# Rotary embedding: the middle batches moved in pairs, 32 KB to a partition

## The chip, the core and the metric

The kernel runs on one core of a Trainium2 chip. Times are device microseconds, with the other cores idle. The span is the profiled execution from the first to the last instruction; the time of the same execution is a little longer (161.94 against 160.5 us in the profiled run of the kernel before). Every ratio below is to runs of the kernel before that were made on the same chip in the same rounds; where the times or traces of two changed kernels are set side by side, they come from different chips unless the text says otherwise. A run of one core is called slow when it took over 1.5% more than the fastest run of the same kernel, the other runs "fast". A difference under 2% counts as "the same".

Names: VectorE (DVE in the profile), GpSimd (POOL), TensorE (PE, with PEld for its weight loads), ScalarE (ACT), SyncE (SP). A line number such as L224 is a line of that kernel's source.

## The reference

```python
# x: (16, 512, 1024) float32, 16 heads of 64; cos, sin: (512, 32)
x = x.reshape(batch, seq, num_heads, head_dim)
x1, x2 = x[..., :half_dim], x[..., half_dim:]
rotated = concatenate([x1 * cos - x2 * sin, x1 * sin + x2 * cos], axis=-1)
```

32 MiB come in and 32 MiB go out. cos and sin depend on the position in the sequence only, so every batch uses the same tables.

## The kernel before

A partition holds 4 consecutive positions ("rows") of a batch: 16 KB that are contiguous in memory. One load and one store of 2 MB serve a batch. For each row VectorE multiplies by cos into PSUM (`mul`), GpSimd multiplies the swapped halves by sin into `t2`, and then the two are added: by VectorE (`comb`), or for 3 rows in 8 by TensorE (an identity matrix times `t2`, accumulated onto the cos product in PSUM), in which case ScalarE copies the sum back. For one row in 8, VectorE also makes the sin product itself.

```python
PE2 = [u % 8 in (1, 3, 6) for u in range(NU)]   # u: rows in order; TensorE adds these
V2 = [u % 8 == 3 for u in range(NU)]            # VectorE makes the sin product of these
NT1 = 3                                         # PSUM slots for cos products
LEAD = 2
...
def on_sync(sp):                                # loads, 10 batches ahead of the stores
    for c in range(NC):
        if c * R >= RING:
            sp.wait_ge(sem_out[c - RING // R], 16)
        sp.dma_start(tile(c), xv[c]).then_inc(sem_in[c], 16)
...
def on_scalar(ae):
    for u in range(NU):
        if PE2[u]:
            ae.wait_ge(sem_e, n_pe[u])
            ae.activation(xs[:, k, :], t1_ps[:, u % NT1, :], COPY).then_inc(sem_a, 1)
        if r == R - 1:                          # last row of the batch
            wait_added(ae, u)
            ae.dma_start(ov[c], tile(c))...     # store
...
def mul(u):                                     # VectorE
    if r == 0:
        ve.wait_ge(sem_in[c], 16)
    if V2[u]:
        ve.tensor_tensor(t2_sb[...], swapped(k), sin_of(s_ps, r), mult)
    if u >= NT1:                                # the PSUM slot of row u - 3 must be free
        ve.wait_ge(sem_a, ...) if PE2[u - NT1] else ve.wait_ge(sem_v, ...)
    ve.tensor_tensor(t1_ps[:, u % NT1, :], x_sb[...], c_ps[...], mult)
...
for u in range(NU + LEAD):                      # VectorE's order: mul(u), then comb(u - 2)
    if u < NU:
        mul(u)
    if u >= LEAD and not PE2[u - LEAD]:
        comb(u - LEAD)
```

## Time and profile before

The median of the first three runs was 161.89 us, of six runs 162.0 us (161.85 to 162.4). The span of the profiled run was 160.5 us.

| what | before |
|---|---|
| DMA, mean over the span | 419 GB/s, full from 8 to 155 us |
| VectorE, GpSimd busy | 82%, 81% |
| GpSimd waits for loads | 8.9 us |
| VectorE waits for ScalarE (a PSUM slot) | 8.6 us |

Lines of the profile page of the kernel before: busy time of the engines, the DMA rows of the span in 40 slices (busy share in tenths, then GB/s), the packets, and three groups of instructions (busy us and mean ns of one, then idle time before them and what ended most of it).

```profile
span 160.5 us, 607 instructions
PE 81.7 (51%) x102; PEld 25.4 (16%) x102; DVE 131.5 (82%) x116; ACT 26.3 (16%) x27; POOL 130.3 (81%) x62
DMA  5999999999999999999999999999999999999996
GB/s 151 404 445 429 433 429 404 412 441 421 433 445 416 441 433 418 441 421 437 431 425 441 421 441 425 433 437 420 441 429 429 433 425 441 429 429 437 421 435 290
DMA packets 4899, 67.27 MB, mean 419 GB/s; under 512 B 544, under 2 KB 800, under 8 KB 800
...
L193 POOL TENSOR_TENSOR t_sb<-x_sb,s_sb 128x1024 f32<-128x1024 f32 x56 | 129.6, 2376 | 17.0 <-DMA x_sb<-in_x_dram 8.9
L224 DVE TENSOR_TENSOR t_ps<-x_sb,tab_ps 128x1024 f32<-128x1024 f32 x64 | 77.1, 1227 | 10.4 <-ACT x_sb L141 8.6
L235 DVE TENSOR_TENSOR x_sb<-t_ps,t_sb 128x1024 f32<-128x1024 f32 x40 | 48.6, 1217 | 0.0
```

The DMA engines do not pause (a share of 1.00 to 1.03 in every stretch of the table from 8 to 155 us). GpSimd has room, and what it waits for is loads. The table by stretches of the kernel before (busy us of each engine, granted TensorE clock, DMA share, GB/s) has a middle piece and the piece near the end:

```profile
core 0: us, PE busy (x) PEld busy (x) DVE busy (x) ACT busy (x) POOL busy (x), PEclk, DMA share, GB/s
60.00:80.00 20.00, 11.38 (x15) 3.14 (x13) 19.64 (x18) 4.09 (x4) 20.00 (x10) 0.71 1.01 431
...
144.20:150.80 6.60, 2.93 (x4) 0.83 (x4) 5.84 (x5) 1.30 (x2) 3.79 (x2) 0.69 1.00 429
```

### The profile page before, as it was taken

What the parts mean: (1) busy time and instruction counts of PE and PEld (TensorE: products, weight loads), DVE (VectorE), ACT (ScalarE), POOL (GpSimd) and SP (SyncE); (2) the same over time, 40 slices, a digit from 0 to 9 for tenths busy, and PEclk for the clock granted to TensorE, in tenths of its full rate; (3) what the DMA queues carried; (4) which work ended last, traced back from release to release, by engine and by line L of the source; (5) the groups of instructions that cost most, each with busy time, mean ns of one, the idle gap of its engine ahead of it and who ended that gap; (6) DMA issues with size and microseconds to landing.
All of it is one profiled execution on the core that took longest, in us unless ns stands there. A gap on an engine that the chain in (4) does not pass through costs nothing.

```text
span 160.5 us, 607 instructions
## 1 busy us (share of the span) xinstructions
PE 81.7 (51%) x102; PEld 25.4 (16%) x102; DVE 131.5 (82%) x116; ACT 26.3 (16%) x27; POOL 130.3 (81%) x62
## 2 busy tenths in 40 slices
PE   6004928354833944854573584575485436576000
PEld 1002402110210220211022021122022002112000
DVE  0089299999999879999999699998999799969400
ACT  3010221122022022012202202211211220220200
POOL 1069999999999999999999993998939988498000
PEclk9999996879595558595765555765567795567555
DMA  5999999999999999999999999999999999999996
GB/s 151 404 445 429 433 429 404 412 441 421 433 445 416 441 433 418 441 421 437 431 425 441 421 441 425 433 437 420 441 429 429 433 425 441 429 429 437 421 435 290
DMA packets 4899, 67.27 MB, mean 419 GB/s; under 512 B 544, under 2 KB 800, under 8 KB 800
## 3 DMA queue, kind: packets, MB, share of 16 engines
q1 hardware_dynamic: 2592, 33.69, 49.9%
q10 hardware_dynamic: 2304, 33.56, 48.8%
q14 instruction: 3, 0.02, 0.0%
HBM read 33.69 MB, written 33.55 MB: 419 GB/s over the span
## 4 chain that ended last, share of the span: by engine, by line
DVE 36%; PE 19%; issue 17%; POOL 10%; ACT 5%; DMA 5%; SPq 0%; DVEq 0%; POOLq 0%
PE t_ps L164 19%; DVE x_sb L235 18%; DVE t_ps L224 15%; POOL t_sb L193 10%; ACT x_sb L141 5%; DMA stage<-in_sin_dram 5%; DVE t_sb L215 4%; SPq L127 0%; SPq L124 0%; ACT s_sb L135 0%; ACT s_sb L136 0%; DVEq L234 0%; DVEq L223 0%; POOLq L116 0%; DVEq L221 0%
## 5 line engine op out<-in xcount | busy, mean ns | idle before, releaser
L193 POOL TENSOR_TENSOR t_sb<-x_sb,s_sb 128x1024 f32<-128x1024 f32 x56 | 129.6, 2376 | 17.0 <-DMA x_sb<-in_x_dram 8.9
L164 PE MATMUL t_ps<-t_sb,ident 128*128 128x512 f32 x96 | 78.9, 972 | 65.8 <-DVE t_ps L224 49.8
L224 DVE TENSOR_TENSOR t_ps<-x_sb,tab_ps 128x1024 f32<-128x1024 f32 x64 | 77.1, 1227 | 10.4 <-ACT x_sb L141 8.6
L235 DVE TENSOR_TENSOR x_sb<-t_ps,t_sb 128x1024 f32<-128x1024 f32 x40 | 48.6, 1217 | 0.0
L141 ACT ACTIVATE x_sb<-t_ps 128x1024 f32<-128x1024 f32 x24 | 24.6, 1023 | 115.8 <-PE t_ps L164 100.9
L164 PEld LDWEIGHTS t_ps<-t_sb,ident 128*128 128x128 f32 x96 | 24.7, 281 | 119.4 <-DVE t_ps L224 86.4
L215 DVE TENSOR_TENSOR t_sb<-x_sb,tab_ps 128x1024 f32<-128x1024 f32 x8 | 9.7, 1210 | 0.0
L202 DVE COPY tab_ps<-stage 128x128 f32<-128x128 f32 x1 | 0.3, 294 | 7.6 <-DMA stage<-in_cos_dram 7.6
L150 PE MATMUL t_ps<-zero 128*128 128x512 bf16 x6 | 2.7, 630 | 1.3 <-DVE zero L198 1.3
L135 ACT ACTIVATE s_sb<-stage 128x128 f32<-128x128 f32 x1 | 0.3, 309 | 6.9 <-DMA stage<-in_sin_dram 6.9
L135 ACT ACT_TABLE_LOAD x1 | 1.3, 1283 | 0.8 <-PEq L268 0.8
L150 PEld LDWEIGHTS t_ps<-zero 128*128 128x128 bf16 x6 | 0.7, 137 | 2.4 <-DVE zero L198 1.2
L198 DVE MEMSET zero<- 128x256 uint32 x1 | 0.3, 272 | 0.9 <-PEq L268 0.9
L175 POOL MEMSET ident<- 128x128 f32 x1 | 0.2, 204 | 0.3 <-POOLq L268 0.3
L177 POOL TENSOR_SCALAR_AFFINE_SELECT ident<-ident 128x128 f32<-128x128 f32 x1 | 0.3, 292 | 0.1
L268 POOL MEMSET const-float32-0.0<- 128x1 f32 x1 | 0.1, 98 | 0.3 <-issue 0.3
L136 ACT ACTIVATE s_sb<-stage 128x128 f32<-128x128 f32 x1 | 0.3, 293 | 0.0
L204 DVE TENSOR_SCALAR tab_ps<-stage 128x128 f32<-128x128 f32 x1 | 0.3, 283 | 0.0
L205 DVE COPY tab_ps<-stage 128x128 f32<-128x128 f32 x1 | 0.3, 283 | 0.0
L268 POOL MEMSET const-bfloat16-1.0<- 128x1 bf16 x1 | 0.1, 101 | 0.0
L268 POOL MEMSET const-uint8-127<- 128x1 uint8 x1 | 0.1, 101 | 0.0
L268 POOL MEMSET const-float32-1.0<- 128x1 f32 x1 | 0.1, 98 | 0.0
## 6 DMA issues: line engine op xcount, KB each, us to landing
x_sb<-in_x_dram SPq DMA_DIRECT2D x16, 2048.0 KB, 52.5
out_dram<-x_sb ACTq DMA_DIRECT2D x16, 2048.0 KB, 19.3
stage<-in_cos_dram SPq DMA_DIRECT2D x1, 64.0 KB, 7.5
stage<-in_sin_dram SPq DMA_DIRECT2D x1, 64.0 KB, 7.2
```

Of the source, the lines that this page charges most:

```text
L135: ae.activation(s_sb[:, :, 0, :], sv, COPY, scale=-1.0)
L136: ae.activation(s_sb[:, :, 1, :], sv, COPY).then_inc(sem_s, 1)
L141: ae.activation(xs[:, k, :], t1_ps[:, u % NT1, :], COPY).then_inc(sem_a, 1)
L150: pe.matmul(t1_ps[:, k, b * BANK:(b + 1) * BANK], zero[:, 0:P], zero[:], start=True, stop=True).then_inc(sem_w, 1)
L164: ins = pe.matmul(t1_ps[:, u % NT1, b * BANK:(b + 1) * BANK], ident[:], t2[:, b * BANK:(b + 1) * BANK], start=False, stop=True, skip_group ...
L177: pl.affine_select(out=ident[:], in_=ident[:], compare_op=mybir.AluOpType.is_equal, fill=0.0, base=0, pattern=[[-1, P]], channel_multiplier=1,
L193: pl.tensor_tensor(t2_sb[:, u % NT2, :, :, :], swapped(k), sin_of(s_sb, r), mult).then_inc(sem_p, 1)
L198: ve.memset(zero[:], 0.0).then_inc(sem_z, 1)
L215: ve.tensor_tensor(t2_sb[:, u % NT2, :, :, :], swapped(k), sin_of(s_ps, r), mult).then_inc(sem_d, 1)
L224: ve.tensor_tensor(t1_ps[:, u % NT1, :].rearrange("p (h d) -> p h d", d=HALF), x_sb[:, k, :, :, :].rearrange("p h t d -> p (h t) d"), c_ps ...
L235: ve.tensor_tensor(xs[:, k, :], t1_ps[:, u % NT1, :], t2_sb[:, u % NT2, :, :, :].rearrange("p h t d -> p (h t d)"), add,).then_inc(sem_v, 1)
L268: nc = _bacc.Bacc("TRN2", target_bir_lowering=False, num_devices=1)
```

## The change

Packets of 32 KB instead of 16 KB should cost the DMA engines less overhead: an estimate from the transfer records of the kernel before, where a line through 27 ns for 512 B and 611 ns for 16 KB leaves 8 ns for a packet itself. 32 KB contiguous bytes are 8 rows, so a batch covers only 64 partitions, and batches 1 to 14 are taken in pairs: partition p holds 8 rows of batch p % 2 of the pair. Batches 0 and 15 stay single, to keep the start and the end short. The pairs need tables in another arrangement; TensorE makes them at the start, by multiplying the single tables with two selection matrices. Core of the diff:

```diff
-    PE2 = [u % 8 in (1, 3, 6) for u in range(NU)]
-    V2 = [u % 8 == 3 for u in range(NU)]
+    tiles = [(0, R1)] + [(b, R2) for b in range(1, batch - 1, 2)] + [(batch - 1, R1)]   # R1 = 4, R2 = 8
+    REGIONS = 5
+    def on_pe(t, r):
+        return r in {0: (1,), NT - 1: (1, 3)}.get(t, (1, 3, 6))
+    V_ROW = {NT - 1: 1}
+    V2 = [t > 0 and r == V_ROW.get(t, 3) for t, r in rows]
...
-        xv = x.rearrange("b (p r) d -> b p (r d)", r=R)
+        x1 = x.rearrange("b (s r) d -> b s (r d)", r=R1)
+        x2 = x.rearrange("b (s r) d -> s b (r d)", r=R2)
...
-                sp.dma_start(tile(c), xv[c]).then_inc(sem_in[c], 16)
+                sp.dma_start(in_sbuf(t), in_dram(x1, x2, t)).then_inc(sem_in[t], 16)   # 4 MB for a pair
...
-                if r == R - 1:
+                if r == tiles[t][1] - 1:          # a pair's store only after its 8th row
                     wait_added(ae, u)
-                    ae.dma_start(ov[c], tile(c))...
+                    ae.dma_start(in_dram(o1, o2, t), in_sbuf(t))...
...
+            for k in range(2):                    # tables of the pairs
+                pe.matmul(pair_ps[:, k]..., pick[:, k]..., stage[:]..., start=True, stop=True)
```

Two things ride along. Loads and stores of the pairs become ready in steps of 4 MB. And the rows were dealt out anew at the ends: VectorE's own sin product moved from row 3 of batch 0 to row 1 of batch 15.

More of the change, by code (lines that the diff above doesn't have):

```diff
@@ L26, in bass_split_heads_rope_kernel @@
     P = 128
-    R = 4
-    assert P * R == seq
+    R1 = seq // P
+    R2 = 2 * R1
+    assert R1 * P == seq and R1 == 4 and batch % 2 == 0
     fp32 = mybir.dt.float32
@@ L34, in bass_split_heads_rope_kernel @@
     COPY = mybir.ActivationFunctionType.Copy
-    RING = 40
-    NC = batch
-    NU = batch * R
-    def where(u):
-        return u // R, u % R, u % RING
-    PE2 = [u % 8 in (1, 3, 6) for u in range(NU)]
-    V2 = [u % 8 == 3 for u in range(NU)]
+    tiles = [(0, R1)] + [(b, R2) for b in range(1, batch - 1, 2)] + [(batch - 1, R1)]
+    NT = len(tiles)
+    REGIONS = 5
+    rows = [(t, r) for t, (_, n) in enumerate(tiles) for r in range(n)]
+    NU = len(rows)
+    def on_pe(t, r):
+        return r in {0: (1,), NT - 1: (1, 3)}.get(t, (1, 3, 6))
+    V_ROW = {NT - 1: 1}
+    PE2 = [on_pe(t, r) for t, r in rows]
+    V2 = [t > 0 and r == V_ROW.get(t, 3) for t, r in rows]
     def count(flags):
@@ L61, in bass_split_heads_rope_kernel @@
     with ExitStack() as stack:
-        x_sb = stack.enter_context(nc.sbuf_tensor([P, RING, H, 2, HALF], fp32))
+        x_sb = stack.enter_context(nc.sbuf_tensor([P, REGIONS * R2, H, 2, HALF], fp32))
         t2_sb = stack.enter_context(nc.sbuf_tensor([P, NT2, H, 2, HALF], fp32))
-        stage = stack.enter_context(nc.sbuf_tensor([P, 2, R * HALF], fp32))
-        s_sb = stack.enter_context(nc.sbuf_tensor([P, R, 2, HALF], fp32))
+        stage = stack.enter_context(nc.sbuf_tensor([P, 2, R1 * HALF], fp32))
+        s1_sb = stack.enter_context(nc.sbuf_tensor([P, R1, 2, HALF], fp32))
+        s2_sb = stack.enter_context(nc.sbuf_tensor([P, R2, 2, HALF], fp32))
         ident = stack.enter_context(nc.sbuf_tensor([P, P], fp32))
+        pick = stack.enter_context(nc.sbuf_tensor([P, 2, P // 2, 2], fp32))
         zero = stack.enter_context(nc.sbuf_tensor([P, BANK], bf16))
         tab_ps = stack.enter_context(nc.psum_tensor([P, BANK], fp32))
+        pair_ps = stack.enter_context(nc.psum_tensor([P, 2, 2, R1, HALF], fp32))
         t1_ps = stack.enter_context(nc.psum_tensor([P, NT1, H * HD], fp32))
-        sem_in = [stack.enter_context(nc.semaphore(f"in{c}")) for c in range(NC)]
-        sem_out = [stack.enter_context(nc.semaphore(f"out{c}")) for c in range(NC - RING // R)]
+        sem_in = [stack.enter_context(nc.semaphore(f"in{t}")) for t in range(NT)]
+        sem_out = [stack.enter_context(nc.semaphore(f"out{t}")) for t in range(NT - REGIONS)]
         sem_rest = stack.enter_context(nc.semaphore("rest"))
@@ L84, in bass_split_heads_rope_kernel, with c_of, s_of, in_dram @@
         sem_e = stack.enter_context(nc.semaphore("pe"))
+        sem_g = stack.enter_context(nc.semaphore("pick"))
+        sem_t = stack.enter_context(nc.semaphore("pairs"))
         sem_a = stack.enter_context(nc.semaphore("act"))
-        c_ps = tab_ps[:, 0:R * HALF].rearrange("p (r d) -> p r d", d=HALF)
-        s_ps = tab_ps[:, R * HALF:R * (HALF + HD)].rearrange("p (r t d) -> p r t d", t=2, d=HALF)
-        xv = x.rearrange("b (p r) d -> b p (r d)", r=R)
-        ov = out.rearrange("b (p r) h d -> b p (r h d)", r=R)
-        xs = x_sb[:].rearrange("p n h t d -> p n (h t d)")
-        def tile(c):
-            k = c * R % RING
-            return x_sb[:, k:k + R].rearrange("p n h t d -> p (n h t d)")
+        c1_ps = tab_ps[:, 0:R1 * HALF].rearrange("p (r d) -> p r d", d=HALF)
+        v_ps = tab_ps[:, R1 * HALF:R1 * HALF + 2 * HD].rearrange("p (k t d) -> p k t d", t=2, d=HALF)
+        def c_of(t, r):
+            return c1_ps[:, r, :] if tiles[t][1] == R1 else pair_ps[:, r // R1, 0, r % R1, :]
+        def s_of(t, r):
+            return s1_sb[:, r] if tiles[t][1] == R1 else s2_sb[:, r]
+        x1 = x.rearrange("b (s r) d -> b s (r d)", r=R1)
+        o1 = out.rearrange("b (s r) h d -> b s (r h d)", r=R1)
+        x2 = x.rearrange("b (s r) d -> s b (r d)", r=R2)
+        o2 = out.rearrange("b (s r) h d -> s b (r h d)", r=R2)
+        xs = x_sb[:].rearrange("p n h t d -> p n (h t d)")
+        def in_dram(single, pairs, t):
+            b, n = tiles[t]
+            return single[b] if n == R1 else pairs[:, b:b + 2, :]
+        def in_sbuf(t):
+            k = t % REGIONS * R2
+            return x_sb[:, k:k + tiles[t][1]].rearrange("p n h t d -> p (n h t d)")
+        def where(u):
+            t, r = rows[u]
+            return t, r, t % REGIONS * R2 + r
         def swapped(k):
             return x_sb[:, k, :, ::-1, :]
-        def sin_of(table, r):
-            return table[:, r, None, :, :].broadcast_to([P, H, 2, HALF])
+        def over_heads(table):
+            return table[:, None, :, :].broadcast_to([P, H, 2, HALF])
         def wait_added(eng, u):
@@ L120, in on_sync @@
         def on_sync(sp):
-            for c in range(NC):
-                if c * R >= RING:
-                    sp.wait_ge(sem_out[c - RING // R], 16)
-                sp.dma_start(tile(c), xv[c]).then_inc(sem_in[c], 16)
-                if c == 0:
+            for t in range(NT):
+                if t >= REGIONS:
+                    sp.wait_ge(sem_out[t - REGIONS], 16)
+                sp.dma_start(in_sbuf(t), in_dram(x1, x2, t)).then_inc(sem_in[t], 16)
+                if t == 0:
                     for i, (table, sem) in enumerate(((cos, sem_cos), (sin, sem_sin))):
-                        sp.dma_start(
-                            stage[:, i, :], table.rearrange("(p r) d -> p (r d)", r=R)
-                        ).then_inc(sem, 16)
-            sp.wait_ge(sem_rest, 16 * (NC - len(sem_out)))
+                        sp.dma_start(stage[:, i, :], table.rearrange("(s r) d -> s (r d)", r=R1)).then_inc(sem, 16)
+            sp.wait_ge(sem_rest, 16 * (NT - len(sem_out)))
         def on_scalar(ae):
@@ L134, in on_scalar @@
             sv = stage[:, 1, :].rearrange("s (r d) -> s r d", d=HALF)
-            ae.activation(s_sb[:, :, 0, :], sv, COPY, scale=-1.0)
-            ae.activation(s_sb[:, :, 1, :], sv, COPY).then_inc(sem_s, 1)
+            ae.activation(s1_sb[:, :, 0, :], sv, COPY, scale=-1.0)
+            ae.activation(s1_sb[:, :, 1, :], sv, COPY).then_inc(sem_s, 1)
+            ae.wait_ge(sem_t, 2)
+            s2 = s2_sb[:].rearrange("p (k r) t d -> p k r t d", r=R1)
+            ae.activation(s2[:, :, :, 0, :], pair_ps[:, :, 1, :, :], COPY, scale=-1.0)
+            ae.activation(s2[:, :, :, 1, :], pair_ps[:, :, 1, :, :], COPY).then_inc(sem_s, 1)
             for u in range(NU):
-                c, r, k = where(u)
+                t, r, k = where(u)
                 if PE2[u]:
@@ L141, in on_scalar @@
                     ae.activation(xs[:, k, :], t1_ps[:, u % NT1, :], COPY).then_inc(sem_a, 1)
-                if r == R - 1:
+                if r == tiles[t][1] - 1:
                     wait_added(ae, u)
-                    ae.dma_start(ov[c], tile(c)).then_inc(sem_out[c] if c < len(sem_out) else sem_rest, 16)
+                    ae.dma_start(in_dram(o1, o2, t), in_sbuf(t)).then_inc(
+                        sem_out[t] if t < len(sem_out) else sem_rest, 16
+                    )
         def on_tensor(pe):
@@ L152, in on_tensor @@
                     ).then_inc(sem_w, 1)
+            pe.wait_ge(sem_g, 3)
+            pe.wait_ge(sem_cos, 16)
+            pe.wait_ge(sem_sin, 16)
+            for k in range(2):
+                pe.matmul(
+                    pair_ps[:, k].rearrange("p c r d -> p (c r d)"),
+                    pick[:, k].rearrange("q s b -> q (s b)"),
+                    stage[:].rearrange("q c f -> q (c f)"),
+                    start=True,
+                    stop=True,
+                ).then_inc(sem_t, 1)
             pe.wait_ge(sem_i, 2)
@@ L185, in on_gpsimd @@
             ).then_inc(sem_i, 1)
-            pl.wait_ge(sem_s, 1)
+            pl.memset(pick[:], 1.0).then_inc(sem_g, 1)
+            pl.wait_ge(sem_g, 1)
+            for k in range(2):
+                pl.affine_select(
+                    out=pick[:, k],
+                    in_=pick[:, k],
+                    compare_op=mybir.AluOpType.is_equal,
+                    fill=0.0,
+                    base=-k,
+                    pattern=[[-2, P // 2], [0, 2]],
+                    channel_multiplier=1,
+                ).then_inc(sem_g, 1)
             for u in range(NU):
@@ L189, in on_gpsimd @@
                     continue
-                c, r, k = where(u)
-                pl.wait_ge(sem_in[c], 16)
+                t, r, k = where(u)
+                if t < 2 and r == 0:
+                    pl.wait_ge(sem_s, t + 1)
+                pl.wait_ge(sem_in[t], 16)
                 wait_t2_free(pl, u)
                 pl.tensor_tensor(
-                    t2_sb[:, u % NT2, :, :, :], swapped(k), sin_of(s_sb, r), mult
+                    t2_sb[:, u % NT2, :, :, :], swapped(k), over_heads(s_of(t, r)), mult
                 ).then_inc(sem_p, 1)
@@ L198, in on_vector, with pair_tables @@
             ve.memset(zero[:], 0.0).then_inc(sem_z, 1)
-            cv = stage[:, 0, :].rearrange("s (r d) -> s r d", d=HALF)
-            sv = stage[:, 1, :].rearrange("s (r d) -> s r d", d=HALF)
             ve.wait_ge(sem_cos, 16)
-            ve.tensor_copy(c_ps, cv)
-            ve.wait_ge(sem_sin, 16)
-            ve.tensor_scalar_mul(s_ps[:, :, 0, :], sv, -1.0)
-            ve.tensor_copy(s_ps[:, :, 1, :], sv).then_inc(sem_c, 1)
+            ve.tensor_copy(c1_ps, stage[:, 0, :].rearrange("s (r d) -> s r d", d=HALF)).then_inc(sem_c, 1)
             ve.wait_ge(sem_c, 1)
             ve.wait_ge(sem_w, NT1 * EH)
+            def pair_tables():
+                sv = V_ROW[NT - 1] * HALF
+                ve.wait_ge(sem_sin, 16)
+                ve.wait_ge(sem_s, 2)
+                for k, row in enumerate((pair_ps[:, 0, 1, 3, :], stage[:, 1, sv:sv + HALF])):
+                    ve.tensor_scalar_mul(v_ps[:, k, 0, :], row, -1.0).then_inc(sem_c, 1)
+                    ve.tensor_copy(v_ps[:, k, 1, :], row).then_inc(sem_c, 1)
+            first_v = V2.index(True)
             def mul(u):
-                c, r, k = where(u)
+                t, r, k = where(u)
                 if r == 0:
-                    ve.wait_ge(sem_in[c], 16)
+                    ve.wait_ge(sem_in[t], 16)
+                if (t, r) == (1, 0):
+                    pair_tables()
+                if u == first_v:
+                    ve.wait_ge(sem_c, 5)
                 if V2[u]:
@@ L215, in mul @@
                     ve.tensor_tensor(
-                        t2_sb[:, u % NT2, :, :, :], swapped(k), sin_of(s_ps, r), mult
+                        t2_sb[:, u % NT2, :, :, :], swapped(k), over_heads(v_ps[:, 1 if t == NT - 1 else 0]), mult
                     ).then_inc(sem_d, 1)
@@ L226, in mul @@
                     x_sb[:, k, :, :, :].rearrange("p h t d -> p (h t) d"),
-                    c_ps[:, r, None, :].broadcast_to([P, 2 * H, HALF]),
+                    c_of(t, r)[:, None, :].broadcast_to([P, 2 * H, HALF]),
                     mult,
@@ L231, in comb @@
             def comb(u):
-                c, r, k = where(u)
+                t, r, k = where(u)
                 ve.wait_ge(sem_m, u + 1)
```

## The prediction

> What bounds the kernel now. The DMA engines. The DMA row of the 40 slices is 9 in all but the first and last; the table by stretches shows a share of 1.00 to 1.03 and 421 to 438 GB/s from 8 us to 155 us of a 160.5 us span. No compute engine is full: VectorE 82%, GpSimd 81%. GpSimd is full from 20 to 80 us, but later waits five times for a load (8.9 us in all): the loads set the pace. 67.27 MB move in any version, so only the rate, the start (about 2 us) and the tail can change. [...]
>
> What the change removes. The records of the transfers have 4,096 packets of 16 KB, 611 ns each at the median, 256 of 512 B at 27 ns and 544 semaphore packets at 9 ns. A line through 512 B and 16 KB gives 0.0368 ns per byte and 8 ns for a packet itself. Pairs turn 3,584 of the 16 KB packets into 1,792 of 32 KB: 112 packets fewer on each of 16 engines, 0.9 us at 8 ns; 224 semaphore packets fewer are 0.1 us more. But completed loads land every 9.73 us while 16 packets pass each engine, 608 ns each, so packets overlap a little: my estimate is 0.6 to 0.8 us, all on the critical path while the DMA engines stay full.
>
> What it adds. Two small matmuls, two masks and small copies (about 0.3 us each), all under the computation of batch 0: no cost, since GpSimd has 9 us of it (four operations of 2.33 us pitch) before the first pair.
>
> What it moves. Loads and stores become ready in steps of 4 MB. I laid out the queues by hand, with 4.84 us per batch at full rate, double while both queues are busy, and 16.3 us of GpSimd for a pair. Batch 0 is stored from about 21.5 us, the first pair's store is issued at about 37.5 us (loads fill the gap). The last pair lands at about 125 us, GpSimd ends it at about 142, its store is issued at about 143.5, with data about 1 us later; the store before it ends at about 144.5, with no load left. So at the end the DMA engines are either just fed or stand idle for up to 2 us: much of the saving can be given back.
>
> Prediction: span about 159.9 us, time 161.2 us, range 159.8 to 163.5. Faster by over 2%: 0.02, within 2%: 0.92, slower by over 2%: 0.06.
>
> What would show it. Right: about 2,880 packets, most of 32 KB and close to 1.21 us; DMA share at 1.0 up to about 143 us; 432 to 434 GB/s in the middle; GpSimd waiting for loads in fewer, longer waits (2 to 4 us); perhaps a DMA dip near 145 us; no wait for the pair tables over 0.5 us. Wrong: 16 KB packets still (no saving), or packets over 1.25 us.
>
> What would make it wrong. [...] Later landings of pairs would add idle DMA time one for one.

The forecast's sum: 160.5 us of span less 0.6 us for the packets gives 159.9 us, and 1.3 us from the span to the time gives 161.2 us. By the packets' 0.6 to 0.8 us of 162 us alone the gain comes to 0.4 to 0.5%.

## More of the kernel before

From the timeline of ScalarE's queue, kernel before: the stores of batches 0, 14 and 15 are issued at

```profile
22.09 0.38 ACTq L144 DMA_DIRECT2D out_dram<-x_sb  x1
...
144.50 0.34 ACTq L144 DMA_DIRECT2D out_dram<-x_sb  x1
...
150.47 0.34 ACTq L144 DMA_DIRECT2D out_dram<-x_sb  x1
```

15 batches in 128.4 us are 8.56 us a batch, 17.1 us for two. The DMA engines need 4.87 us for 2 MB (431 GB/s), so 19.5 us for the loads and the stores of two batches. Computation is a little faster than the transfers, and everything ready waits in the queues (19.3 us from issue to landing for a store, at the median).

Timeline of the kernel before:

```profile
52.24 3.78 PE L164 MATMUL t_ps<-t_sb,ident 128*128 128x512 f32 x4 [2.76 <-DVE t_ps L224]
...
56.06 1.02 ACT L141 ACTIVATE x_sb<-t_ps 128x1024 f32<-128x1024 f32 x1 [5.52 <-PE t_ps L164]
...
57.11 1.23 DVE L224 TENSOR_TENSOR t_ps<-x_sb,tab_ps 128x1024 f32<-128x1024 f32 x1 [1.41 <-ACT x_sb L141]
```

TensorE takes 3.78 us for its row at a granted clock of 0.50, ScalarE drains it in 1.02 us, and VectorE, which needs that PSUM slot three rows later, stood idle for 1.41 us.

## The result, and the profile after

The kernel after took 168.31 us (median of 6 runs, 167.53 to 168.97) against 162.0 us. The ratio is 1.0387 (95% interval 1.0357 to 1.0416), slower. Ratios here are the mean time of one kernel's fast runs over that of the other's of the same rounds, so they are not quite the ratios of the medians quoted.

The page of the kernel after:

```profile
span 166.3 us, 596 instructions
PE 87.1 (52%) x106; PEld 27.4 (16%) x106; DVE 131.9 (79%) x118; ACT 27.0 (16%) x29; POOL 132.3 (80%) x65
DMA  5999989999998999999999999999999999608897
GB/s 146 474 421 410 473 378 430 426 457 410 422 497 386 457 426 388 473 402 467 410 457 418 418 465 394 465 402 473 394 430 426 430 473 402 268 0 378 378 430 327
DMA packets 2882, 67.26 MB, mean 404 GB/s; under 512 B 320, under 2 KB 576, under 8 KB 576
...
L251 POOL TENSOR_TENSOR t_sb<-x_sb,s_sb 128x1024 f32<-128x1024 f32 x56 | 129.9, 2356 | 14.5 <-DVE x_sb L302 7.4
```

The packets are as planned: 2,882 of them, and in the transfer records (the start, length and size of every packet in the trace) a packet of 32 KB takes 1,213 ns at the median where two of 16 KB take 2 x 611. No compute operation became slower (GpSimd 2,356 ns after 2,376; VectorE's cos product 1,227 ns in both). But the DMA row has a hole: a slice with no bytes at all, in the last eighth. The table by stretches of the kernel after, for the stretch that was full before:

```profile
144.20:150.80 6.60, 3.17 (x5) 1.09 (x4) 6.46 (x6) 1.02 (x1) 3.29 (x2) 0.76 0.00 0
```

No packet starts in these 6.6 us. (The tables count a packet by its start. By the transfer records the last packets before the hole ended at 145.2 us and the next began at 151.05 us, so all engines stood idle together for 5.9 us, and one engine for 6.7 us on the mean.) The timeline of ScalarE's queue in the kernel after tells why: these are the stores of batch 0, of the first, the last but one and the last pair, and of batch 15.

```profile
24.11 0.38 ACTq L175 DMA_DIRECT2D out_dram<-x_sb  x1
42.03 0.62 ACTq L175 DMA_DIRECT2D out_dram<-x_sb  x1
...
130.78 0.55 ACTq L175 DMA_DIRECT2D out_dram<-x_sb  x1
149.84 0.55 ACTq L175 DMA_DIRECT2D out_dram<-x_sb  x1
156.54 0.34 ACTq L175 DMA_DIRECT2D out_dram<-x_sb  x1
```

All loads were in, the store of the pair before ended at 145.2 us, and the last pair's store was issued at 149.84 us; its data moves from 151.05 us. The seven pairs were stored every 17.96 us on average ((149.84 - 24.11) / 7), where the prediction had reckoned with 16.3. The waits of the kernel after (us in all, times, longest):

```profile
POOL t_sb L251 <- DVE x_sb L302: 7.4, 6, 2.6
...
DVE t_ps L291 <- ACT x_sb L172: 8.6, 7, 1.4
...
DVE tab_ps L267 <- DMA x_sb<-in_x_dram: 3.7, 1, 3.7
```

In this run GpSimd waits for no load of a pair; it waits for VectorE to free `t2` slots. (On another chip, below, GpSimd did wait for loads, twice, while VectorE waited for none of them and the last pair was late all the same.) So computation, not the loads, set the time of the last pair, and within computation VectorE, which waits once in each of the seven pairs: 1.4 us in five of them, 0.6 and 0.9 us in the others. Timeline of the kernel after, inside one pair:

```profile
45.38 2.35 DVE L291 TENSOR_TENSOR t_ps<-x_sb,pair_ps 128x1024 f32<-128x1024 f32 x2
...
46.66 3.78 PE L208 MATMUL t_ps<-t_sb,ident 128*128 128x512 f32 x4 [2.00 <-DVE t_ps L291]
47.64 1.22 DVE L302 TENSOR_TENSOR x_sb<-t_ps,t_sb 128x1024 f32<-128x1024 f32 x1
...
48.89 1.23 DVE L291 TENSOR_TENSOR t_ps<-x_sb,pair_ps 128x1024 f32<-128x1024 f32 x1
50.48 1.02 ACT L172 ACTIVATE x_sb<-t_ps 128x1024 f32<-128x1024 f32 x1 [4.76 <-PE t_ps L208]
51.53 1.23 DVE L291 TENSOR_TENSOR t_ps<-x_sb,pair_ps 128x1024 f32<-128x1024 f32 x1 [1.41 <-ACT x_sb L172]
```

Row 3 goes to TensorE when its cos product is done (46.66). Until the cos product of row 6, which needs the same PSUM slot, VectorE has three operations (the cos product of row 4, the sum of row 2, the cos product of row 5), 3.5 us of work. TensorE and ScalarE need 4.8 us. A row's four matmuls take 3.78 us where the granted clock is 0.50 (here, and at 52 us in the kernel before) and 1.98 us where it is 1.00 (at 153 us here, at 128 us in the kernel before). The same 1.41 us stood in the trace before, where nothing depended on it (ratio 0.9996 with TensorE almost without work, below).

Theories at this point. **S**: the store of a pair is one step of 4 MB that is ready only after eight rows, and near the end no other transfer is left. **W**: the pace of VectorE, with its waits, makes the last pair late. **L**: the 3.7 us wait for the first pair's 4 MB at the start delays all that follows. **R**: the rows dealt out anew at the ends. Rivals: **T**, the tables or the interleaved pattern; **P**, 32 KB packets themselves.

### The profile page after: what moved, and what is told of

It reads as the page before. It is cut to its first block, busy times and chain, and to the rows that moved or that the text cites. A ratio compares the mean times of both kernels' runs of the same rounds, so it can differ in the third digit from the quotient of the medians.

```text
span 166.3 us, 596 instructions
## 1 busy us (share of the span) xinstructions
PE 87.1 (52%) x106; PEld 27.4 (16%) x106; DVE 131.9 (79%) x118; ACT 27.0 (16%) x29; POOL 132.3 (80%) x65
## 2 busy tenths in 40 slices
DMA packets 2882, 67.26 MB, mean 404 GB/s; under 512 B 320, under 2 KB 576, under 8 KB 576
## 4 chain that ended last, share of the span: by engine, by line
DVE 37%; PE 23%; issue 19%; ACT 7%; DMA 4%; POOL 3%; SPq 0%; DVEq 0%
PE t_ps L208 23%; DVE x_sb L302 20%; DVE t_ps L291 13%; ACT x_sb L172 7%; DVE t_sb L282 4%; DMA stage<-in_sin_dram 4%; POOL t_sb L251 3%; SPq L156 0%; SPq L153 0%; ACT s_sb L162 0%; ACT s_sb L163 0%; DVEq L290 0%; DVEq L145 0%
## 5 line engine op out<-in xcount | busy, mean ns | idle before, releaser
L251 POOL TENSOR_TENSOR t_sb<-x_sb,s_sb 128x1024 f32<-128x1024 f32 x56 | 129.9, 2356 | 14.5 <-DVE x_sb L302 7.4
L208 PE MATMUL t_ps<-t_sb,ident 128*128 128x512 f32 x96 | 82.3, 1007 | 62.0 <-DVE t_ps L291 53.3
L291 DVE TENSOR_TENSOR t_ps<-x_sb,pair_ps 128x1024 f32<-128x1024 f32 x56 | 67.8, 1227 | 10.2 <-ACT x_sb L172 8.6
L302 DVE TENSOR_TENSOR x_sb<-t_ps,t_sb 128x1024 f32<-128x1024 f32 x40 | 48.7, 1218 | 0.0
L208 PEld LDWEIGHTS t_ps<-t_sb,ident 128*128 128x128 f32 x96 | 25.5, 293 | 118.6 <-DVE t_ps L291 93.1
L291 DVE TENSOR_TENSOR t_ps<-x_sb,tab_ps 128x1024 f32<-128x1024 f32 x8 | 9.6, 1227 | 0.2
L282 DVE TENSOR_TENSOR t_sb<-x_sb,tab_ps 128x1024 f32<-128x1024 f32 x8 | 9.7, 1211 | 0.0
L190 PE MATMUL pair_ps<-stage,pick 128*128 128x256 f32 x4 | 2.0, 667 | 5.2 <-DMA stage<-in_sin_dram 5.2
L190 PEld LDWEIGHTS pair_ps<-stage,pick 128*128 128x128 f32 x4 | 1.2, 324 | 6.2 <-issue 6.0
L234 POOL TENSOR_SCALAR_AFFINE_SELECT pick<-pick 128x128 f32<-128x128 f32 x2 | 1.4, 704 | 0.1
L166 ACT ACTIVATE s_sb<-pair_ps 128x256 f32<-128x256 f32 x1 | 0.4, 383 | 1.7 <-PE pair_ps L190 1.7
L167 ACT ACTIVATE s_sb<-pair_ps 128x256 f32<-128x256 f32 x1 | 0.4, 378 | 0.0
```

The costliest lines, as they stand in the source:

```text
L166: ae.activation(s2[:, :, :, 0, :], pair_ps[:, :, 1, :, :], COPY, scale=-1.0)
L167: ae.activation(s2[:, :, :, 1, :], pair_ps[:, :, 1, :, :], COPY).then_inc(sem_s, 1)
L190: pe.matmul(pair_ps[:, k].rearrange("p c r d -> p (c r d)"), pick[:, k].rearrange("q s b -> q (s b)"), stage[:].rearrange("q c f -> q (c f)"),
L208: ins = pe.matmul(t1_ps[:, u % NT1, b * BANK:(b + 1) * BANK], ident[:], t2[:, b * BANK:(b + 1) * BANK], start=False, stop=True, skip_group ...
L234: pl.affine_select(out=pick[:, k], in_=pick[:, k], compare_op=mybir.AluOpType.is_equal, fill=0.0, base=-k, pattern=[[-2, P // 2], [0, 2]], ...
L251: pl.tensor_tensor(t2_sb[:, u % NT2, :, :, :], swapped(k), over_heads(s_of(t, r)), mult).then_inc(sem_p, 1)
```

## The experiments

### Steps of 4 MB in the kernel before, with 16 KB packets and the old tables

```diff
+    if c % 2 == 1 and c < NC - 1: pl.wait_ge(sem_in[c + 1], 16)   # VectorE likewise, at row 0
...
+    if c % 2 == 1 and c < NC - 1: continue                        # no store yet
+    for e in ((c,) if c in (0, NC - 1) else (c - 1, c)):           # both of the pair
+        ae.dma_start(ov[e], tile(e))...
```

> The kernel before, with 16 KB per partition and its own tables, but with the waits of pairs: VectorE and GpSimd start the first batch of a pair (1-2, 3-4, ... 13-14) only when both loads have landed, and both stores are issued when the second batch is done. Theory S (the steps of readiness cost the time: the last pair's store is issued too late, about 150 us, and VectorE starts late): span 165 to 167 us and a stretch of about 5 us without DMA near 145 us. Rival T (the 32 KB packets or the pair tables cost it): span 160.5 to 161.5 us, as before.

Measured: of six runs, three had spans of 165.7 to 166.0 us (slow, 168.53 to 168.87 us) and three 160.5 to 161.7 us (fast, 162.18 to 164.6 us; ratio 1.0119). The profiled run was a slow one: its last pair's store is issued at 149.64 us, and a slice near 145 us moves 4 GB/s. So a hole can appear without 32 KB packets and without the new tables, but it does so in half of the runs only, and those are called slow. The run is inconclusive by itself: the fast runs alone lie near what T expected (160.5 to 161.5 us) and not where S did (165 to 167). T is decided by the runs with row 5 below.

### The kernel after with 16 KB packets

```diff
-    sp.dma_start(in_sbuf(t), in_dram(x1, x2, t)).then_inc(sem_in[t], 16)
+    for h in range(2):                                            # rows 0 to 3, rows 4 to 7
+        sp.dma_start(half_sbuf(t, h), half_dram(x2, t, h)).then_inc(sem_in[t], 16)
...
+    # stores likewise; every wait is for both halves
```

> The kernel after, with each pair's load and store issued as two transfers of 16 KB per partition, but both waited for and released together, so steps and tables stay. Theory S: span within 0.7 us of 166.3, because the end is set by when the last pair is computed. Rival P (packets of 32 KB themselves slow the end): span 160.5 to 162.5 us.

Measured: 167.4 us, ratio 1.0303; spans of the fast runs 163.6, 164.8 and 166.5, of the slow one 166.4. Rival P falls as the cause: with small packets the fast runs stay 3% slower than the kernel before, and none came to the 160.5 to 162.5 us that P expected. The spread is wider than S expected; on this chip the span varied from run to run.

### The last pair's store in two halves

```diff
+    if t == NT - 2 and r in (R1 - 1, R2 - 1):
+        h = r // R1
+        wait_added(ae, u)
+        ae.dma_start(half_dram(o2, t, h), half_sbuf(t, h)).then_inc(sem_rest, 16)
```

> The kernel after, with only the last pair's store issued in two halves: rows 0 to 3 when they are done (about 140.5 us), rows 4 to 7 as before (149.8 us). Theory S: the idle stretch near 145 us fills except for about 1.5 us; then the last batch's store, still issued at 156.5 us, ends it: span 162.5 to 163.5 us. If VectorE's late start did not matter, the DMA engines would be full to the end: span about 160. Rival T: 166.3 us.

Measured: 163.89 us (163.63 to 164.16), ratio 1.0115; spans 161.6 to 161.8, a little less than S expected. The profile page and the timeline of ScalarE's queue of this run:

```profile
DMA  5999999999999999999999999999989999989977
```

```profile
138.98 0.55 ACTq L185 DMA_DIRECT2D out_dram<-x_sb  x1
148.54 0.55 ACTq L185 DMA_DIRECT2D out_dram<-x_sb  x1
155.24 0.35 ACTq L188 DMA_DIRECT2D out_dram<-x_sb  x1
```

The hole is gone (DMA share 0.98 from 140 to 148 us), although the second half is issued nearly as late as the whole was. S holds: it takes the 4 MB step to make the hole. What remains, the last batch's store at 155.24 us against 150.47 before, is lateness of computation.

### The first pair's load in two halves

```diff
+    if t == 1:
+        for h, sem in enumerate((sem_in[1], sem_in1b)):
+            sp.dma_start(half_sbuf(1, h), half_dram(x2, 1, h)).then_inc(sem, 16)
+    # rows 0 to 3 wait for sem_in[1], rows 4 to 7 for sem_in1b
```

> The kernel after, with only the first pair's load issued in two halves with a semaphore each. VectorE's wait of 3.7 us for it at 15 us should vanish. Theory L (that wait delays all later stores, because VectorE's order bounds the pace and not GpSimd's): batch 0's store is issued at about 22 instead of 24.1 us, the last pair's at 146 to 147.5 instead of 149.8, span 163 to 164.3 us. Rival (GpSimd sets the pace, which did not wait there): unchanged, 165.8 to 166.6 us.

Measured: 167.66 us, ratio 1.0267; spans 163.5 and 164.8 (fast), 166.2 and 166.6 (slow). On the same chip the run with 16 KB packets, which keeps the wait, had 163.6, 164.8 and 166.5: no gain, although the first of them alone would have fitted L. Batch 0's store is issued at 24.08 us in the profiled run (a slow one; only its first 25 us are read here), as in the kernel after. Timeline of VectorE in this run:

```profile
19.25 1.23 DVE L307 TENSOR_TENSOR t_ps<-x_sb,pair_ps 128x1024 f32<-128x1024 f32 x1 [3.82 <-ACT x_sb L186]
```

The wait for the load has become a wait of the same length for ScalarE, at the same place: TensorE's first row, whose sin product GpSimd delivered at 14.3 us, holds the PSUM slot. Theory L falls. A wait that the profile shows is not the cause of a delay if another one ends at the same time.

### TensorE almost without work (wrong result on purpose)

```diff
-    ident[:], t2[:, b * BANK:(b + 1) * BANK],
+    zero[:, 0:P], zero[:],                                        # bf16; all waits stay
```

> The kernel after, with TensorE multiplying a bf16 zero block instead of adding the products (wrong result on purpose; all waits stay): about 0.9 us instead of 3.8 us of TensorE work for each of its rows. Theory W (the pace of VectorE, which waits for TensorE and ScalarE at the low granted clock, makes the last pair late): pairs are stored every 16.3 to 16.7 us instead of 17.9, the last pair's store is issued before 142 us, no idle DMA stretch, span 159.5 to 160.5 us. If steps alone cost it, whatever the pace: the store stays near 149 us and the span near 166.

The 0.9 us is an estimate: the six bf16 products of this shape at the start of the kernel before took 2.74 us together, at a granted clock of 1.00, and a row has two.

Measured: 163.18 us, ratio 1.0074; spans 161.7 to 162.1. The first five pairs are stored every 16.4 us; then GpSimd waits for loads (5.8 us). Stores of the last pair and of batch 15, timeline of ScalarE's queue:

```profile
142.83 0.55 ACTq L175 DMA_DIRECT2D out_dram<-x_sb  x1
148.58 0.35 ACTq L175 DMA_DIRECT2D out_dram<-x_sb  x1
```

No hole. The pace of 16.4 us is what the prediction had assumed for the kernel as it is, and over five pairs in a row it appears only in this run, with TensorE's light products. W holds. Two details miss what W expected: the last pair's store came at 142.83 us and not before 142, and the span is still 1.2 us longer than before (160.5 us or less was expected). In this run the last transfer's 16 parts (16 landing records to a transfer) landed 2.6 us apart, against 1.0 us in the kernel before; that this is the 1.2 us is likely and not tested.

### The rows at the ends as in the kernel before

```diff
-    return r in {0: (1,), NT - 1: (1, 3)}.get(t, (1, 3, 6))
-    V2 = [t > 0 and r == V_ROW.get(t, 3) for t, r in rows]
+    return r in {0: (1, 3), NT - 1: (2,)}.get(t, (1, 3, 6))
+    V2 = [r == 3 and t not in (NT - 1,) for t, r in rows]
```

> The kernel after, with batch 0 and batch 15 giving their rows to the engines as the kernel before does: VectorE's extra product for row 3 of batch 0 again and none in batch 15, TensorE rows 1 and 3 of batch 0 and row 2 of batch 15. Theory R (the moved row costs GpSimd one operation of 2.33 us at the start and VectorE 1.2 us before the last pair's last sum): batch 0's store at about 22.1 us instead of 24.1, the last pair's at 146.3 to 147.5 instead of 149.8, idle DMA 2 to 3 us instead of 6, span 162.8 to 164 us. If the row order doesn't matter: 166.2 us.

Measured: 165.73 us (163.67 to 166.3, one of four slow), ratio 1.0189 (1.0118 to 1.026, so unclear at 2%); spans of the fast runs 162.3, 163.7 and 164.0. In the profiled run batch 0's store is issued at 22.48 us and the last pair's at 143.56, earlier than R had it, and there is no hole; this run also had the highest granted clock of the four (0.722). R holds for the start (1.6 us). Its share at the end stands in the trace of the kernel after, where VectorE's own product for batch 15 (L282) comes before the last sum of the last pair (L302):

```profile
146.27 1.22 DVE L282 TENSOR_TENSOR t_sb<-x_sb,tab_ps 128x1024 f32<-128x1024 f32 x1
...
148.54 1.22 DVE L302 TENSOR_TENSOR x_sb<-t_ps,t_sb 128x1024 f32<-128x1024 f32 x1
```

There the last pair took 19.06 us, 1.3 us more than the six before it on the mean (17.78); with the rows as before it took 16.63 us, no more than the others. The remaining 3.4 of the 6.3 us by which the last pair's store came earlier go with shorter waits of VectorE for ScalarE (4.9 us in all, 8.6 in the kernel after). How much of that is the rows and how much the run's clock is not separated.

### Rows as before and the last store in halves

This is the sum of the two diffs above.

> The last pair's store in two halves and the rows as before, together. Theories S and R together: first half issued at about 138 us, no idle DMA, last batch's store at about 153.5 us; span 160 to 161 us against 161.7 with the halves alone.

Measured: two of four runs slow. The fast ones took 163.26 and 163.54 us (spans 161.9 and 161.2), ratio 1.0087. R had expected 160 to 161 us of span; it is no better than the halves alone (1.0115), within their intervals. The profiled run was slow (span 166.5), and there the 16 parts of a transfer landed up to 8.4 us apart.

### Four single batches

```diff
-    tiles = [(0, R1)] + [(b, R2) for b in range(1, batch - 1, 2)] + [(batch - 1, R1)]
+    tiles = [(0, R1), (1, R1)] + [(b, R2) for b in range(2, batch - 2, 2)] + [(batch - 2, R1), (batch - 1, R1)]
+    # rows of the single batches as in the kernel before
```

> A candidate for a better kernel: batches 0, 1, 14 and 15 single with 16 KB per partition and the kernel before's rows, pairs of 32 KB only for batches 2 to 13. Theory S with R: the steps at the start and the end are those of the kernel before, DMA full to the end, and 1,536 packets of 32 KB save about 0.5 us: span 159.8 to 160.6 us (before 160.6). If the 4 MB steps in the middle already cost it: 162 us or more.

Measured: 163.12 us, ratio 1.0092; spans 160.6 to 162.0. No hole, but the last store is issued at 153.84 us, and the last two slices of the DMA row show 8 and 7 tenths. That fits S, and the pace remains; but the rows changed as well, so this run does not test S alone.

### VectorE's own product at row 5 of a pair

```diff
-    V2 = [t > 0 and r == V_ROW.get(t, 3) for t, r in rows]
+    V2 = [t > 0 and r == V_ROW.get(t, 5) for t, r in rows]
-    ... pair_ps[:, 0, 1, 3, :] ...                                # its table
+    ... pair_ps[:, 1, 1, 1, :] ...
+    if V2[u]: ve.wait_ge(sem_d, n_dve[u])                         # in comb
```

> The kernel after with one edit, and right results: VectorE makes the product of row 5 of each pair instead of row 3. In the traces VectorE waits 1.41 us for ScalarE before the product of row 6 (TensorE row 3 to be drained), with three operations in between; now four lie in between. Theory W (pace): the 1.4 us waits shrink to about 0.3, pairs are stored every 17.0 to 17.4 us instead of 17.9, the last pair's store is issued at 144.5 to 147 us, span 161.5 to 164.5. If the pace doesn't matter: 166.3 us.

Measured: 162.64 us (162.26 to 164.0), ratio 1.0053, results right. The edit gives VectorE a fourth operation between the cos products of rows 3 and 6. Page, waits and timeline of this run:

```profile
DMA  5999999999999999999999999999999999999997
```

```profile
DVE t_ps L291 <- ACT x_sb L172: 2.4, 7, 0.8
```

```profile
66.85 1.23 DVE L291 TENSOR_TENSOR t_ps<-x_sb,pair_ps 128x1024 f32<-128x1024 f32 x1 [0.40 <-ACT x_sb L172]
...
143.66 0.55 ACTq L175 DMA_DIRECT2D out_dram<-x_sb  x1
```

The wait of 1.41 us is now 0.40. All waits for ScalarE fell from 8.6 to 2.4 us, by 6.2. The last pair's store came 6.2 us earlier (149.84 to 143.66), and the span fell by 6.0. (That waits and store moved by the same 6.2 us is chance: on one chip, below, 5.0 us less of waits brought the store 3.7 us forward.) The DMA row is full. Steps of 4 MB, tables, interleaved pattern and packets are all as in the kernel after, so T and P fall, and W is the cause that decides.

### Four single batches with row 5

> The candidate with four single batches, and row 5 as in the run beside it. Theory W with S: last store issued at 149 to 152 us instead of 153.8, DMA full to the end, span 159.3 to 160.3 us, time 160.8 to 162 us (before 162.0). If 32 KB packets bring nothing to the slowest DMA engine: span 160.5 to 161.5.

Measured: 162.74 us (162.03 to 163.23), ratio 1.0035 (1.0006 to 1.0064); spans 159.9 to 160.8. The last store is issued at 150.17 us. The spans are those of the kernel before on this chip (160.6 to 160.8), or a little less; the times are not.

### Two controls with TensorE almost without work (wrong results on purpose)

Four single batches:

> The candidate with four single batches, with TensorE's light zero block (wrong result on purpose), so that computation is early and the DMA engines alone set the end. If the 1.0 us that the packets save in mean time per engine reaches the end: 159.3 to 159.8 us of span, 0.7 to 1.2 us less than the control beside it. If the slowest engine takes it back (last transfers landing over 2 us apart): 160.5 or more.

The 1.0 us stands in the transfer records: packets of 16 and 32 KB took 157.8 us of each engine on the mean in the kernel before and 156.8 us in the kernel after.

The kernel before:

> Control: the kernel before with TensorE's light zero block (wrong result on purpose). It is bound by DMA with slack in its computation, so every theory expects its span unchanged, 160.2 to 160.8 us; if it gets faster, computation did bound it.

Measured: the control did not move, 162.08 us, ratio 0.9996, so the pace of computation costs the kernel before nothing. The other gave three slow runs of four (165.3 to 165.9 us of span, the 16 parts of a transfer landing up to 7.5 us apart) and one of 161.8. It does not answer its question.

### The same chip: kernel after, row 5, and row 5 with 16 KB packets

The kernel after again:

> The kernel after, unchanged, as a control on the same chip as the two runs beside it. Theory W expects what was seen before: span 165.5 to 166.7 us, idle DMA near 145 us. If this chip makes it as fast as the row-5 kernel was (160.3), then the row was not the cause and the chip or its granted clock was.

Row 5 again:

> The kernel after with VectorE's product at row 5 of a pair, beside the control. Theory W: span 160 to 161.5 us, 4.5 to 6 us less than the control.

Row 5 with each pair's transfers as two of 16 KB per partition:

> The row-5 kernel with each pair's load and store as two transfers of 16 KB per partition, waited for together: only the packets differ from the run beside it. If the 9 ns that a 32 KB packet saves over two of 16 KB reach the end: this one is 0.5 to 1.0 us slower. If not: within 0.4 us, or faster.

Measured: kernel after 166.75 us (165.93 to 166.82, ratio 1.0273), row 5 162.48 us (162.16 to 163.03, ratio 1.0025), row 5 with 16 KB packets 163.21 us (162.76 to 163.66, ratio 1.0061). Spans of the kernel after were 163.9 to 164.8, a little less than on the first chip. The same stretch in the tables of the first two, kernel after and then row 5:

```profile
143.00:148.50 5.50, 1.92 (x3) 0.83 (x3) 5.36 (x6) 1.02 (x1) 2.96 (x2) 0.81 0.25 107
```

```profile
143.00:148.50 5.50, 4.06 (x5) 1.46 (x6) 5.43 (x6) 1.02 (x1) 0.46 (x1) 0.50 0.75 322
```

DMA share 0.25 against 0.75, packets counted by their start. It is not the granted clock: the six runs of row 5 had mean clocks of 0.632 to 0.712, and the two at 0.632 (162.47 and 162.76 us) beat every run of the kernel after (0.667 to 0.713). In this pair of profiled runs VectorE's waits for ScalarE fell from 7.4 to 2.4 us, the last pair's store came at 144.59 instead of 148.31 us and the span was 3.7 us shorter (4.5 to 6 us were expected). The waits in these two runs, kernel after (two lines) and then row 5 (us in all, times, longest):

```profile
DVE t_ps L291 <- ACT x_sb L172: 7.4, 6, 1.4
POOL t_sb L251 <- DMA x_sb<-in_x_dram: 3.8, 2, 3.0
...
DVE t_ps L291 <- ACT x_sb L172: 2.4, 11, 0.8
```

With 32 KB packets row 5 is 0.67 us faster than with 16 KB packets (the difference of the mean times, 163.20 and 162.53; the mean spans differ by 0.4 us). Both profiled runs still ran dry for about 1 us before the last pair's store, and with 16 KB packets every transfer of a pair is also issued twice, so what the packets alone save while the DMA engines are full to the end is not shown.

### The candidate: rows as before and row 5

> Candidate: the kernel after with VectorE's product at row 5 of a pair, and batches 0 and 15 with the kernel before's rows. From the runs with one of these each: batch 0's store at about 22.3 us, pairs every 17.0 us, the last pair's store issued by 142.5 us, before the store ahead of it ends, so no idle DMA; the packets' 0.6 us then show: span 159.3 to 160.2 us, time 161.0 to 161.9 us against 162.0 before. If something else of the pairs costs time: 162.2 us or more.

With the last pair's store in halves as well:

> The same candidate with the last pair's store in two halves. If the last pair's step still costs anything in the run beside it, this is 0.3 to 1 us faster; if the DMA engines are already full to the end, equal within 0.3 us.

Measured: 162.48 us (one of six slow; ratio 1.0018, interval 0.9983 to 1.0052) and 162.53 us (ratio 1.0031, 0.9997 to 1.0065), against 162.05 us before. Single fast runs reach 161.6 us, but neither beats the kernel before. In the second the DMA row is full and the span 160.2 us. By the first one's own expectation (162.2 us or more) something else of the pairs still costs time. It is not in the span: that of its fast runs is 160.4 us on the mean, against 160.7 before. It stays open. The loss can be undone; a gain was not found.

## Why the prediction was wrong

| point of the prediction | measured |
|---|---|
| DMA bounds the kernel, packets 2,880, 32 KB in 1.21 us | right: 2,882, 1.213 us |
| packets save 0.6 to 0.8 us where DMA is full | the size agrees, in part by luck: 0.67 us (row 5, 32 against 16 KB), where the DMA engines were not full to the end |
| tables, computation per row: no cost | right: the same mean times; row 5 keeps the tables |
| 16.3 us of computation for a pair | **wrong: 17.96 us** |
| batch 0's store at 21.5 us | 24.1 us (the rows dealt out anew; 21.8 to 22.5 with the old rows) |
| last pair's store at 143.5 us, idle up to 2 us | **149.84 us, idle 6.6 us** |
| GpSimd waits for loads, fewer and longer | not in the profiled run, where it waits for VectorE and never for a load of a pair; on another chip twice, up to 3.0 us; in neither was it what made the last pair late |
| 161.2 us, 159.8 to 163.5 | 168.31 us |

The step that failed is "16.3 us of GpSimd for a pair". It took the engine that was busy without a break from 20 to 80 us as the one that sets the pace, and multiplied its operation by seven. But GpSimd was also running ahead within its six `t2` slots, and VectorE was the slower one: it was busy 16.3 to 16.6 us in each of the first six pairs, as long as GpSimd, and its waits of up to 1.41 us for TensorE and ScalarE came on top. So a pair took 17.78 us, and 17.96 with the last pair and its additional product. The prediction knew that the end stood on an edge ("later landings of pairs would add idle DMA time one for one") but put the danger in the loads, which came in time. Seven pairs at 1.66 us more are 11.6 us; part of it was hidden, because the prediction had let pairs wait for loads and so gave them 122.0 us (143.5 - 21.5) in all, where they took 125.7. That is 3.7 us; batch 0's later store adds 2.6; together the last pair's store came 6.3 us late (149.84 - 143.5). The span was 6.4 us over the predicted one, and the rest of the 7.1 us is that the time exceeds the span by 2.0 us in the kernel after and by 1.4 us in the kernel before. No view shows where those 0.6 us are spent, and they stay open; the kernels derived from the one after show 1.4 to 2.6 us, and those with light TensorE 1.3.

Numbers of the profile before would have told the pace. Two batches were stored every 17.1 us, although computation was at times held up by loads; and the waits listed 8.6 us of VectorE for ScalarE. They looked harmless, because in that kernel they are: taking them away changed nothing (ratio 0.9996). They cost time only once a store of 4 MB had to be ready at a given moment. In the fast profiled runs where the DMA engines ran dry, the span is the issue of the last pair's store plus 16.5 us:

| run (the profiled one) | last pair's store, us | span, us | difference |
|---|---|---|---|
| kernel after | 149.84 | 166.3 | 16.5 |
| kernel after, other chip | 148.31 | 164.8 | 16.5 |
| row 5, that chip | 144.59 | 161.1 | 16.5 |
| row 5 with 16 KB packets, that chip | 144.99 | 161.6 | 16.6 |
| light TensorE (never dry) | 142.83 | 161.7 | 18.9 |

Three batches' stores at 4.87 us are 14.6 us, and the data of the last pair's store starts 1.2 us after its issue; the rest is the end of the last transfer. So in these runs, until the DMA engines stay full, every microsecond by which the last pair's store comes earlier is a microsecond of the span (on one chip 148.31 to 144.59 us, and 164.8 to 161.1).

So there are two causes and it needs both: the 4 MB step at the end (taken away alone: ratio 1.0387 to 1.0115, on another chip) and the pace (mended alone: from 1.0273 to 1.0025 on one chip). The rows dealt out anew make it worse: they add 1.6 us at the start and, by the trace, some 1.3 us in the last pair; no run takes away the latter alone.

## What to carry to other kernels

The kernel before, with the DMA engines full and its compute engines at 81 and 82%, lost nothing to the pace of its computation while the pieces were 2 MB (control: ratio 0.9996); with pieces of 4 MB, and the rows at the ends dealt out anew, the kernel was 2.7 to 3.9% slower. Before making the pieces larger, work out when the last large store can be issued, from the rhythm at which the stores were issued in the trace and not from the operation times of the busiest engine. Count an engine's waits in: VectorE, busy for 79% of the span of the kernel after where GpSimd showed 80%, set the pace of 17.78 us with its waits of up to 1.41 us. And keep the last pieces small: larger packets were worth 0.67 us here, a late last piece over 6.

## What else the traces show

- Larger pieces: 4 MB steps instead of 2 MB, together with the pace of computation, cost 2.7 to 3.9% here. In the kernel after no packet started in 6.6 us near the end; on the other chip the DMA share was 0.25 in the 5.5 us shown above. The larger packets brought 0.67 us.
- Packets: one of 32 KB took 9 ns less than two of 16 KB (2 x 611 - 1,213 ns, medians of the transfer records of the kernel after).
- Queues with unequal packets: while batch 0's store (16 KB packets) ran beside pair loads (32 KB) in the kernel after, the loads' queue started 114 of its packets and the store's queue 112 in 12.8 us (28.95 to 41.75 us), so 3.74 MB of loads and 1.84 MB of the store. There the queue with the smaller packets got the smaller share.
- Landings: the 16 parts of one transfer landed up to 2.1 us apart in the kernel before, up to 3.4 us in the fast profiled runs with 32 KB packets (four single batches; 2.4 in the kernel after, 2.6 with light TensorE), and 7.5 and 8.4 us in two slow runs with 32 KB packets. Why the last parts come late there is open.
